# FFN gate and up of 18 of 22 tiles by seven products of quarters, with weight sums made by accumulating transfers

## The chip, the cores and the metric

The kernel runs on one core of a Trainium2 chip. The metric is the device time of one launch in microseconds; times are given as the median of several runs, and one further execution is recorded by the hardware profiler. Names used below: PE is TensorE (PEld its weight loads), DVE VectorE, ACT ScalarE, POOL GpSimd and SP SyncE, whose queue only starts transfers here.

## The reference

A decoder trunk of two layers on 512 tokens of 1024 channels: layer 0 mixes with a state-space model, layer 1 with stick-breaking attention; each is followed by the same kind of gated FFN, and a norm ends it. The change is in the FFN:

```
D_MODEL, SEQ, DEPTH, D_FF, CONV_W = 1024, 512, 2, 2816, 3

def conv_ffn(h, w_up, conv_w, conv_b, w_down):
    gu = h @ w_up
    g = gu[..., :D_FF]
    u = gu[..., D_FF:]
    g = conv_general_dilated(g, conv_w, padding=[(CONV_W - 1, 0)], feature_group_count=D_FF) + conv_b
    return (silu(g) * u) @ w_down

x = x + conv_ffn(rms_norm(x, norm_ffn[layer]), w_up[layer], conv_w[layer], conv_b[layer], w_down[layer])
```

## The kernel before

Everything is held channel by token: `x` is a tile of 128 partitions by 8 (the `k` of 1024 channels) by 512 tokens. A float32 product is made of three matmuls in fp32r: each operand is split into a high part (a cast by ACT, `split_hi`) and a low part (raw minus high, a DVE subtraction, `split_lo`), and `gemm` adds high x high, high x low and low x high in a bank of PSUM. Weights come from HBM into a `raw` tile (`load_raw`, by SP's queue), three of these in turn; their high and low parts have three buffers each (pool `wp`, tags `hi` and `lo`).

An FFN (`ffn`, `ffn_body`) has 22 tiles `f` of 128 hidden channels. For each, the gate's product `fg` and the up's `fu` run over 8 k with all 512 columns, 24 matmuls each. `rb` is the reciprocal root of the norm, one row per token; since the raw residual is what is multiplied (its high and low parts `xs`, made while the stage before ends), DVE multiplies `fg` and `fu` by `rb`. Then follow the causal convolution (`acc`: one ACT step, two DVE steps on 511 and 510 columns), silu on ACT (`s`), the product `u` and its split into `ah` and `al`, kept in `acts`. The 22 tiles go in three chunks of 8, 7 and 7 (`FF_CHUNKS`). After each chunk come eight downs `fd`, one per 128 output channels, each over the chunk's tiles, three matmuls a tile, and `x` gets `fd` added. After the last chunk of a layer each finished `x[:, n]` goes to the next stage (`st_next`); in layer 1 the last two downs are done by `Final.last` in halves of 256 tokens, in an order written by hand.

The order of the work on the engines is otherwise set by a scheduler, which puts an instruction ahead of others where it expects an operand sooner; each engine then runs its list strictly in order. Only in `Final.last`, and in the attention's loop, is the order that of the code. The seven banks of tag `b` are handed out in turn.

Of the kernel before, what the change touches and what calls it, by code (L numbers as in the profile page):

```python
# [47 lines left out]
def trunk(ctx: ExitStack, tc: tile.TileContext, A, out):  # L48
# [764 lines left out]


    def ffn(layer, prev, st_next):
        with Work(f"ff{layer}", {"g": "la", "s": "lb", "u": "lc"}, a=24, acc=2, y=1, half=6):
            banks_by_tag(b=7, st=1)
            rb, _ = prev.st.finish()
            ffn_body(layer, prev.xs, rb, st_next)

    def ffn_body(layer, xs, rb, st_next):
        cw = const.tile([P, FT, 4], F32, name="cw")
        nc.scalar.dma_start(out=cw, in_=A["conv"][layer])
        for ci, (f0, f1) in enumerate(FF_CHUNKS):
            acts = []
            for f in range(f0, f1):
                wg = load_split(A["w_up"][layer, f, 0], 8, name="wg")
                bg = B("fg")
                gemm(bg, wg, xs)
                wu = load_split(A["w_up"][layer, f, 1], 8, name="wu")  # L830
                bu = B("fu")
                gemm(bu, wu, xs)
                g = T("g", tag="g")
                tt(g, bg, rb, MUL)
                acc = T("acc", tag="acc")
                SC.activation(out=acc, in_=g, func=AF.Identity, scale=cw[:, f, 2:3], bias=cw[:, f, 3:4])  # L836
                stt(acc[:, 1:], g[:, :S - 1], cw[:, f, 1:2], acc[:, 1:], MUL, ADD)
                stt(acc[:, 2:], g[:, :S - 2], cw[:, f, 0:1], acc[:, 2:], MUL, ADD)
                s = T("s", tag="s")
                SC.activation(out=s, in_=acc, func=AF.Silu)  # L840
# [3 lines left out]
                ah, al = T("ah", F32R, "a"), T("al", F32R, "a")
                SC.copy(out=ah, in_=u)
                tt(al, u, ah, SUB)
                acts.append((ah, al))
            for n in range(KT):
                w = load_split(A["w_dn"][layer, n][:, f0 * P:f1 * P], f1 - f0, name="wd")
                if f1 == FT and n == KT - 2 and hasattr(st_next, "last"):  # L850
                    st_next.last((w, load_split(A["w_dn"][layer, KT - 1][:, f0 * P:f1 * P], f1 - f0, name="wd")), acts)
                    return
                bd = B("fd")
                gemm(bd, w, acts)
                tt(x[:, n], x[:, n], bd, ADD)
                if ci == len(FF_CHUNKS) - 1:
                    st_next(n)
# [498 lines left out]
    class Final:  # L1356
# [7 lines left out]
        def __call__(self, n):  # L1364
            self.st.add(n)
            if n == 0:
                tc.keep_in_program_order(SC.preload_act_table_set("abs_reciprocal_sqrt_and_small"))
                self.y = wide("yo", KT, "y").rearrange("p (k t) -> p k t", k=KT)
            SC.activation(out=self.y[:, n], in_=x[:, n], func=AF.Copy, scale=gcol(NFIN, n))

        def last(self, ws, acts):
            n0, H, K = KT - 2, S // 2, len(acts)
            halves = [slice(0, H), slice(H, S)]
            sq6, sq7, v, r, q, rr = (T(t, tag="half") for t in ("sq6", "sq7", "v7", "r7", "q7", "rr7"))
# [16 lines left out]

            def root(i):
                c = halves[i]
                SC.activation(out=r[:, c], in_=total[:, c], func=AF.Abs_reciprocal_sqrt, scale=1.0 / 1024.0, bias=self.eps)
# [134 lines left out]
```

## Time and profile before

| | |
|---|---|
| median of three runs | 1229.2 us (1228.55 to 1229.86) |
| the profiled execution: whole time | 1230.19 us |
| its span, first to last instruction | 1228.4 us |
| first FFN / second FFN in the chain of waits | 228.9 to 584.2 us / 866 to the end, about |
| TensorE clock granted, mean | 0.998 |
| transfers | 118.47 MB, 96 GB/s over the span |

The profile's views used below: the page (busy shares, the chain of waits by line, the costliest groups), the chain in order of time (start, length, engine, line and count), groups by shape (count, busy time, mean ns of one, idle time of the engine ahead of them and what ended it), windows (busy time of each engine in a stretch) and the timeline (start, length, instruction). A matmul's duration there is from its issue to its modelled end and overlaps the next; what a stream costs is read from start to start.

### The profile page before, as it was taken

The numbers are of one execution on the slowest core, as the hardware profiler recorded it, in microseconds if no ns is written. First come the engines' busy times: TensorE is split into PE (matmuls) and PEld (weight loads), VectorE is DVE, ScalarE is ACT, GpSimd is POOL, SyncE is SP. The second block draws the span as 40 slices with busy tenths as digits, with TensorE's granted clock in tenths as the row PEclk, the third lists the DMA queues.
The fourth block names the chain that finished last, engine by engine and source line by source line (L and its number), as shares of the span: only waits on it lengthen the run. The fifth ranks groups of instructions, "written<-read, shape, count | busy, mean of one in ns | idle before, by whom it ended". The sixth has DMA issues, their size and how long they took to land.

```text
span 1228.4 us, 16234 instructions
## 1 busy us (share of the span) xinstructions
PE 1204.6 (98%) x6434; PEld 984.1 (80%) x6434; DVE 804.0 (65%) x1254; ACT 546.0 (44%) x881; POOL 24.0 (2%) x65
## 2 busy tenths in 40 slices
PE   7999999999999999999999999999999999999996
PEld 3467788788888888888889898988888888888885
DVE  7999665655445635657878989878655346536554
ACT  5245453433223323334577878765433233313341
POOL 1011010000000000000000000000000000000000
PEclk9999999999999999999999999999999999999999
DMA  5565342223333233233211211123233332332322
GB/s 195 157 174 146 111 136 89 89 98 103 89 100 103 81 108 103 87 96 104 68 52 54 82 52 51 39 86 103 87 103 93 96 103 85 91 116 86 97 76 69
DMA packets 55037, 118.47 MB, mean 96 GB/s; under 512 B 12881, under 2 KB 28497, under 8 KB 54961
## 3 DMA queue, kind: packets, MB, share of 16 engines
q1 hardware_dynamic: 50304, 105.02, 28.2%
q0 software_dynamic: 3248, 11.54, 3.1%
q8 instruction: 50, 0.82, 0.3%
q10 hardware_dynamic: 1408, 0.88, 0.2%
q14 instruction: 27, 0.21, 0.1%
HBM read 109.03 MB, written 8.39 MB: 96 GB/s over the span
## 4 chain that ended last, share of the span: by engine, by line
PE 88%; DVE 8%; ACT 1%; issue 1%; DMA 1%; DVEq 0%; SPq 0%; ACTq 0%
PE fu L112 19%; PE fd L112 19%; PE fg L112 19%; PE gl L112 6%; PE kqb L112 6%; PE ob L112 5%; PE z L112 5%; PE v L112 4%; PE u L112 2%; DVE k L118 2%; DVE p L118 1%; PE y L112 1%; DMA x<-in_xT 1%; DVE cm L118 1%; ACT xg L282 1%
## 5 line engine op out<-in xcount | busy, mean ns | idle before, releaser
L112 PE MATMUL fd<-ah,wdh 128*128 128x512 f32 (+1 forms) x366 | 140.0, 382 | 0.0
L112 PE MATMUL fd<-al,wdh 128*128 128x512 f32 (+1 forms) x366 | 139.4, 381 | 0.0
L112 PE MATMUL fd<-ah,wdl 128*128 128x512 f32 (+1 forms) x366 | 139.4, 381 | 0.0
L118 DVE TENSOR_TENSOR x<-x,fd 128x512 f32<-128x512 f32 (+1 forms) x50 | 33.3, 665 | 116.6 <-PE fd L112 116.6
L163 ACT CAST wuh<-wur 128x1024 fp32r<-128x1024 f32 x44 | 46.3, 1053 | 134.0 <-PE fg L112 117.8
L163 ACT CAST wdh<-wdr 128x896 fp32r<-128x896 f32 (+1 forms) x48 | 47.2, 983 | 123.8 <-PE fd L112 91.5
L118 DVE TENSOR_TENSOR g<-fg,rb 128x512 f32<-128x512 f32 x44 | 30.4, 691 | 96.3 <-PE fg L112 93.6
L112 PE MATMUL fu<-xh,wuh 128*128 128x512 f32 x220 | 86.0, 391 | 0.0
L112 PE MATMUL fg<-xh,wgl 128*128 128x512 f32 x220 | 85.7, 389 | 0.0
L112 PE MATMUL fu<-xl,wuh 128*128 128x512 f32 x220 | 85.6, 389 | 0.0
L112 PE MATMUL fg<-xh,wgh 128*128 128x512 f32 x220 | 85.6, 389 | 0.0
L112 PE MATMUL fu<-xh,wul 128*128 128x512 f32 x220 | 85.6, 389 | 0.0
L112 PE MATMUL fg<-xl,wgh 128*128 128x512 f32 x220 | 85.6, 389 | 0.0
L118 DVE TENSOR_TENSOR u<-fu,rb 128x512 f32<-128x512 f32 x44 | 30.4, 691 | 80.5 <-PE fu L112 80.5
L112 PE MATMUL fu<-xhl,wuh 128*128 128x512 f32 x264 | 81.9, 391 | 0.0
L112 PE MATMUL fg<-xhl,wgh 128*128 128x512 f32 x264 | 81.6, 389 | 0.0
L112 PEld LDWEIGHTS fd<-ah,wdh 128*128 128x128 f32 x366 | 68.8, 188 | 13.3
L112 PEld LDWEIGHTS fd<-ah,wdl 128*128 128x128 f32 x366 | 68.8, 188 | 13.3
L112 PEld LDWEIGHTS fd<-al,wdh 128*128 128x128 f32 x366 | 68.8, 188 | 13.2
L163 ACT CAST wgh<-wgr 128x1024 fp32r<-128x1024 f32 x44 | 46.3, 1053 | 70.1 <-PE fd L112 32.6
L112 PE MATMUL u<-xg,wi 128*128 128x512 f32 x128 | 64.0, 635 | 7.3 <-ACT xg L282 7.3
L115 DVE SCALAR_TENSOR_TENSOR acc<-g,cw,acc 128x511 f32<-128x511 f32 x88 | 65.7, 747 | 2.5 <-ACT acc L836 0.9
(250 smaller groups left out, 2798.0 us busy)
## 6 DMA issues: line engine op xcount, KB each, us to landing
wgr<-in_w_up SPq DMA_DIRECT2D x44, 512.0 KB, 3.5
wur<-in_w_up SPq DMA_DIRECT2D x44, 512.0 KB, 3.5
wdr<-in_w_dn SPq DMA_DIRECT2D x32, 448.0 KB, 3.3
wdr<-in_w_dn SPq DMA_DIRECT2D x16, 512.0 KB, 3.5
wvr<-in_w_glu POOLq DMA_DIRECT2D x12, 512.0 KB, 3.8
ks<-kx SPq DMA_DIRECT2D x32, 128.0 KB, 2.5
m<-ks SPq DMA_DIRECT2D x8, 512.0 KB, 4.3
awr<-in_w_k SPq DMA_DIRECT2D x8, 512.0 KB, 3.4
```

The costliest lines, as they stand in the source:

```text
L112: PE.matmul(o, lhsT=lhsT, rhs=rhs, start=start, stop=stop, skip_group_check=True)
L115: (eng or V).scalar_tensor_tensor(out=o, in0=a, scalar=s, in1=b, op0=op0, op1=op1)
L118: (eng or V).tensor_tensor(out=o, in0=a, in1=b, op=op)
L163: SC.copy(out=hi, in_=raw)
L282: SC.activation(out=xg.rearrange("p (j c) -> p j c", j=8), in_=by_step(x[:, k]), func=AF.Copy, scale=gcol(NMIX0, k))
```

## The change

Four of the 22 tiles (the first chunk) are computed as before. The other 18 are computed by Strassen's scheme with seven products instead of eight. The 2x2 blocks are: rows gate and up, inner halves k 0 to 3 and k 4 to 7, columns tokens 0 to 255 and 256 to 511. Each of the seven products is 4 k x 3 matmuls of 256 columns (`prod`), two products a bank: `up1` and `gate2` in bank `f0`, `m17` and `n6` in `f1`.

- The seven sums of quarters of the activations, already normed (times gain and `rb`), are made once a layer by `make_forms(k)`, one call after each of the first chunk's four tiles, and split into `fh` and `fl` (DVE and ACT). They use the same three blocks (`block`, tag `sr`) that later hold the weight sums.
- The weight sums `wsa` and `wsb` are made by transfers (`summed`): SP's queue copies one quarter twice side by side into a block, and POOL's queue then adds the two diagonal quarters into it with an accumulating transfer, which waits for the copy. The diagonal quarters themselves (`wdg`) are a third transfer, and their difference `d` is a DVE subtraction. Each of `wsa`, `wdg`, `wsb` (1024 wide) and `d` (512 wide) is split into a high and a low part.
- The products are combined on DVE in halves of 256 (`t`, `wv`, `u`, `g`), with two copies from PSUM by ACT; no multiplication by `rb` is left in these tiles.
- The chunks are now 4, 5, 4, 5 and 4 tiles (`FF_ENDS`), so 40 downs a layer instead of 24 with the same number of matmuls. Three downs of the first chunk follow it at once (`LEAD`); the others stand between the products of the next chunk's tiles (`between`, twice a tile); the last chunk's eight come at the end.
- `acts` takes 8 buffers of its own and, in every other chunk, those of `xs` (tag `ta`). `Final` takes its tiles from the space of the forms, and `last` has its hand-written cuts moved, since the last chunk has 4 k instead of 7.

```
-FF_CHUNKS = ((0, 8), (8, 15), (15, 22))
+FF_ENDS = (4, 9, 13, 18, 22)
+LEAD = 3
...
+        def make_forms(k):
+            q, c = (block(n).rearrange("p (s c) -> p s c", s=4) for n in ("fq", "fc"))
+            for i, kk in ((1, k), (0, k + 4)):
+                stt(q[:, i::2], x[:, kk].rearrange("p (s c) -> p s c", s=2), gcol(NFFN0 if layer == 0 else NFFN1, kk),
+                    rb.rearrange("p (s c) -> p s c", s=2), MUL, MUL)
+            tt(c[:, 0:2], bc(q[:, 1], 1, [P, 2, H]), q[:, 2:4], ADD)
+            tt(c[:, 2], q[:, 3], q[:, 2], SUB)
+            tt(c[:, 3], q[:, 0], q[:, 2], ADD)
+            tt(q[:, 0], q[:, 0], q[:, 1], SUB)
+            for src, s in ((q[:, 0:3], slice(0, 3)), (c, slice(3, 7))):
+                SC.copy(out=fh[:, k, s], in_=src)
+                tt(fl[:, k, s], src, fh[:, k, s], SUB)
...
+            def summed(rows, half, name):
+                t = block(name)
+                t2 = t.rearrange("p (h c) -> p h c", h=2)
+                nc.sync.dma_start(out=t2, in_=quarters(rows, half, 0))
+                GP.dma_start(out=t2, in_=quarters(0, 0, diag), accum_op=ADD)
+                return t
...
+            def prod(o, wt, s, first=False, last=True):
+                gemm(o, wt, [(fh[:, k, s], fl[:, k, s]) for k in range(4)], k1=4, first=None if first else False, last=None if last else False)
+
+            s1 = split_w(summed(1, 0, "wsa"), 8, "wsa")
+            b0, b1 = B("f0"), B("f1")
+            up1, gate2, m17, n6 = b0[:, 0:H], b0[:, H:], b1[:, 0:H], b1[:, H:]
+            prod(up1, part(s1, 1), 1, True, False)
+            raw = wr.tile([P, 8 * P], F32, tag="raw", name="wdg", bufs=3)
+            nc.sync.dma_start(out=raw.rearrange("p (h c) -> p h c", h=2), in_=quarters(0, 0, diag))
+            r = split_w(raw, 8, "wdg")
+            prod(gate2, part(r, 0), 5, False, False)
+            d = fp.tile([P, S], F32, tag="d", name="d", bufs=1)
+            tt(d, raw[:, 0:4 * P], raw[:, 4 * P:], SUB)
...
+            prod(m17, (dh, dl), 3, True, False)
+            prod(n6, part(s1, 0), 4)
...
+            between(0)
+            prod(up1, part(r, 1), 0)
+            s2 = split_w(summed(0, 1, "wsb"), 8, "wsb")
+            prod(gate2, part(s2, 0), 2)
+            prod(m17, part(s2, 1), 6)
...
+            finish_act(f, g, mul, acts, tag)
+            between(1)
...
+            for f in range(f0, f1):
+                if ci == 0:
+                    up(f, acts, tag)
+                    make_forms(f)
+                else:
+                    up7(f, acts, tag, between)
+            todo = [(ci, n, acts) for n in range(KT)]
+            if ci == 0:
+                for _ in range(LEAD):
+                    down(*todo.pop(0))
```

How the instructions stand before and after is shown at three places. First, PE in an FFN, where a tile's gate ends and its up begins, before:

```order
L112 MATMUL fg<-xh,wgl 128x512
L112 MATMUL fg<-xhl,wgh 128x512 x2
L112 MATMUL fg<-xhl,wgl 128x512
L112 MATMUL fg<-xhl,wgh 128x512 x2
L112 MATMUL fg<-xhl,wgl 128x512
L112 MATMUL fg<-xhl,wgh 128x512 x2
L112 MATMUL fg<-xhl,wgl 128x512
L112 MATMUL fu<-xh,wuh 128x512
L112 MATMUL fu<-xl,wuh 128x512
L112 MATMUL fu<-xh,wul 128x512
```

And after, in the second tile of the second chunk, where the product `n6` (bank `f1`, here `f_2831`) ends and a down of the first chunk follows:

```order
L117 MATMUL f_2831<-fh,wsah 128x256
L117 MATMUL f_2831<-fl,wsah 128x256
L117 MATMUL f_2831<-fh,wsal 128x256
L117 MATMUL fd<-ah,wdh 128x512
L117 MATMUL fd<-al,wdh 128x512
L117 MATMUL fd<-ah,wdl 128x512
```

Matmuls of 512 columns have become matmuls of 256 with the same three parts, and a down now stands in the middle of a tile. Second, DVE in the first chunk, where no such work stood before; a tile there had, before, these rows (`wul` and `wgl` are low parts of weights, `al` of the activation):

```order
L118 TENSOR_TENSOR u<-u,s 128x512
L118 TENSOR_TENSOR wgl<-wgr,wgh 128x1024
L118 TENSOR_TENSOR al<-u,ah 128x512
L118 TENSOR_TENSOR g<-fg,rb 128x512
L118 TENSOR_TENSOR wul<-wur,wuh 128x1024
L115 SCALAR_TENSOR_TENSOR acc<-g,cw,acc 128x511
L115 SCALAR_TENSOR_TENSOR acc<-g,cw,acc 128x510
L118 TENSOR_TENSOR u<-fu,rb 128x512
```

and after, where the third tile's weights are split (`fq` and `fc` are the sums of quarters, `fl` their low parts):

```order
L123 TENSOR_TENSOR u_2410<-u_2410,s_2408 128x512
L123 TENSOR_TENSOR fc_2418<-fq_2417 128x256
L123 TENSOR_TENSOR wgl_2433<-wgr_2429,wgh_2431 128x1024
L123 TENSOR_TENSOR al_2414<-u_2410,ah_2413 128x512
L123 TENSOR_TENSOR fq_2417<-fq_2417 128x256
L123 TENSOR_TENSOR fl_2250<-fc_2418,fh_2249 128x1024
L123 TENSOR_TENSOR fl_2250<-fq_2417,fh_2249 128x768
L123 TENSOR_TENSOR wul_2464<-wur_2460,wuh_2462 128x1024
```

The steps of make_forms stand between those of the tile, the forms of the second call ahead of `wul`. Third, DVE in a seven-product tile of the second chunk:

```order
L123 TENSOR_TENSOR x<-x,fd 128x512
L123 TENSOR_TENSOR wsal<-wsa,wsah 128x1024
L123 TENSOR_TENSOR wdgl<-wdg,wdgh 128x1024
L123 TENSOR_TENSOR tw<-tw,f_2674 128x256 x2
L123 TENSOR_TENSOR g<-f_2675,tw 128x256
L123 TENSOR_TENSOR wdl<-wdr,wdh 128x512
L120 SCALAR_TENSOR_TENSOR acc<-g,cw,acc 128x511
L120 SCALAR_TENSOR_TENSOR acc<-g,cw,acc 128x510
L123 TENSOR_TENSOR tw<-f_2830,m_2892 128x256
L123 TENSOR_TENSOR u<-f_2674,s 128x256
L123 TENSOR_TENSOR u<-u,s 128x256
L123 TENSOR_TENSOR d<-wdg 128x512
```

The next tile's two low parts (`wsal`, `wdgl`) stand behind the addition to x and ahead of the steps that make this tile's gate (`tw`, `g`); `wsbl`, the last of the three, stands four rows further.

More of the change, by code (lines that the diff above doesn't have):

```diff
@@ L100, in wide, with forms_tile @@
         return pool.tile([P, n * S], F32, tag=tag, name=name, bufs=bufs[tag])
+    def forms_tile(name, dt=F32):
+        pool, bufs = cur["w"]
+        return pool.tile([P, 7 * 4 * (S // 2)], dt, tag="fo", name=name, bufs=bufs["fo"])
     def N(name, tag, bufs):
@@ L815, in ffn @@
     def ffn(layer, prev, st_next):
-        with Work(f"ff{layer}", {"g": "la", "s": "lb", "u": "lc"}, a=24, acc=2, y=1, half=6):
+        with tc.tile_pool(name=f"fd{layer}", bufs=1) as fp, \
+                Work(f"ff{layer}", {"g": "la", "s": "lb", "u": "lc"}, a=8, acc=2, fo=2):
             banks_by_tag(b=7, st=1)
             rb, _ = prev.st.finish()
-            ffn_body(layer, prev.xs, rb, st_next)
-    def ffn_body(layer, xs, rb, st_next):
+            ffn_body(layer, prev.xs, rb, st_next, fp)
@@ L822, in ffn_body, with block, finish_act, up @@
+    def ffn_body(layer, xs, rb, st_next, fp):
         cw = const.tile([P, FT, 4], F32, name="cw")
         nc.scalar.dma_start(out=cw, in_=A["conv"][layer])
[L824 to L840, printed above, removed]
+        H = S // 2
+        chunks = [(f, n) for f, n in zip((0,) + FF_ENDS, FF_ENDS)]
+        fh, fl = (forms_tile(n, F32R)[:, :7 * 4 * H].rearrange("p (k s c) -> p k s c", k=4, s=7) for n in ("fh", "fl"))
+        def block(name):
+            return fp.tile([P, 8 * P], F32, tag="sr", name=name, bufs=3)
+        def make_forms(k):
[10 more added lines that the diff above has]
+                tt(fl[:, k, s], src, fh[:, k, s], SUB)
+        def finish_act(f, g, mul, acts, tag):
+            acc = T("acc", tag="acc")
+            SC.activation(out=acc, in_=g, func=AF.Identity, scale=cw[:, f, 2:3], bias=cw[:, f, 3:4])
+            stt(acc[:, 1:], g[:, :S - 1], cw[:, f, 1:2], acc[:, 1:], MUL, ADD)
+            stt(acc[:, 2:], g[:, :S - 2], cw[:, f, 0:1], acc[:, 2:], MUL, ADD)
+            s = T("s", tag="s")
+            SC.activation(out=s, in_=acc, func=AF.Silu)
+            u = mul(s)
+            ah, al = T("ah", F32R, tag), T("al", F32R, tag)
+            SC.copy(out=ah, in_=u)
+            tt(al, u, ah, SUB)
+            acts.append((ah, al))
+        def up(f, acts, tag):
+            wg = load_split(A["w_up"][layer, f, 0], 8, name="wg")
+            bg = B("fg")
+            gemm(bg, wg, xs)
+            wu = load_split(A["w_up"][layer, f, 1], 8, name="wu")
+            bu = B("fu")
+            gemm(bu, wu, xs)
+            g = T("g", tag="g")
+            tt(g, bg, rb, MUL)
+            def mul(s):
@@ L843, in ffn_body @@
                 tt(u, u, s, MUL)
[L844 to L857, printed above, removed]
+                return u
@@ new lines, in up, with up7, quarters, part @@
+            finish_act(f, g, mul, acts, tag)
+        def up7(f, acts, tag, between):
+            w = A["w_up"][layer, f]
+            def quarters(rows, half, step):
+                o = w[rows, :, half * 4 * P:half * 4 * P + 4 * P]
+                return bass.AP(o.tensor, o.offset, [[KT * P, P], [step, 2], [1, 4 * P]])
+            diag = P * KT * P + 4 * P
+            def summed(rows, half, name):
[4 more added lines that the diff above has]
+                return t
+            def part(wt, h):
+                return [t[:, h * 4 * P:h * 4 * P + 4 * P] for t in wt]
+            def prod(o, wt, s, first=False, last=True):
[10 more added lines that the diff above has]
+            tt(d, raw[:, 0:4 * P], raw[:, 4 * P:], SUB)
+            dh, dl = (fp.tile([P, S], F32R, tag=n, name=n, bufs=2) for n in ("dh", "dl"))
+            SC.copy(out=dh, in_=d)
+            tt(dl, d, dh, SUB)
+            prod(m17, (dh, dl), 3, True, False)
+            prod(n6, part(s1, 0), 4)
+            m, tw, u = (T(n, tag="u") for n in ("m3", "tw", "u"))
+            t, wv = tw[:, 0:H], tw[:, H:]
+            SC.copy(out=m[:, 0:H], in_=gate2)
+            tt(t, up1, m[:, 0:H], ADD)
+            tt(wv, m17, t, ADD)
+            tt(u[:, H:], n6, wv, SUB)
+            between(0)
[3 more added lines that the diff above has]
+            prod(m17, part(s2, 1), 6)
+            g = T("g", tag="g")
+            tt(t, t, up1, SUB)
+            SC.copy(out=g[:, H:], in_=gate2)
+            tt(t, t, gate2, SUB)
+            tt(g[:, 0:H], m17, t, ADD)
+            def mul(s):
+                tt(u[:, 0:H], up1, s[:, 0:H], MUL)
+                tt(u[:, H:], u[:, H:], s[:, H:], MUL)
+                return u
+            finish_act(f, g, mul, acts, tag)
+            between(1)
@@ new lines, in down @@
+        def down(ci, n, acts):
+            f0, f1 = chunks[ci]
+            w = load_split(A["w_dn"][layer, n][:, f0 * P:f1 * P], f1 - f0, name="wd")
+            if f1 == FT and n == KT - 2 and hasattr(st_next, "last"):
+                st_next.last((w, load_split(A["w_dn"][layer, KT - 1][:, f0 * P:f1 * P], f1 - f0, name="wd")), acts)
+                return True
+            bd = B("fd")
+            gemm(bd, w, acts)
+            tt(x[:, n], x[:, n], bd, ADD)
+            if f1 == FT:
+                st_next(n)
@@ new lines, in ffn_body, with between @@
+        todo = []
+        for ci, (f0, f1) in enumerate(chunks):
+            acts, tag = [], ("a", "ta")[ci % 2]
+            slots = 2 * (f1 - f0)
+            n0, count = len(todo), [0]
+            def between(i):
+                count[0] += 1
+                while todo and (n0 - len(todo)) * slots < count[0] * n0:
+                    down(*todo.pop(0))
[8 more added lines that the diff above has]
+                for _ in range(LEAD):
+                    down(*todo.pop(0))
@@ L860, in attention @@
+        for job in todo:
+            if down(*job):
+                return
     def attention(prev, st_next):
@@ L1373, in last @@
             halves = [slice(0, H), slice(H, S)]
-            sq6, sq7, v, r, q, rr = (T(t, tag="half") for t in ("sq6", "sq7", "v7", "r7", "q7", "rr7"))
+            half = forms_tile("half")
+            sq6, sq7, v, r, q, rr = (half[:, i * S:i * S + S] for i in range(6))
             sq = {n0: sq6, n0 + 1: sq7}
@@ L1421, in last @@
                 mm(total[:, halves[0]], ones, acc[:, halves[0]], True, False)
-                product(n0, 1, 0, 5)
+                product(n0, 1, 0, 3)
                 mm(total[:, halves[0]], ones, sq[n0 + 1][:, halves[0]], False, True)
                 root(0)
-                product(n0, 1, 5, K)
+                product(n0, 1, 3, K)
                 newton(0)
@@ L1430, in last @@
                 send(0, 0, 4, nc.sync)
-                product(n0 + 1, 1, 0, 4)
+                product(n0 + 1, 1, 0, 2)
                 mm(total[:, halves[1]], ones, acc[:, halves[1]], False, False)
-                product(n0 + 1, 1, 4, K)
+                product(n0 + 1, 1, 2, K)
                 added(n0 + 1, 1)
```

2 lines of the change are left out of this document (1 added, 1 removed).

## The prediction

> **What bounds the kernel now.** I read the page's share table first, then the chain that ended last in order of time, then windows of the two kinds of FFN stretch, then groups by shape.
>
> ```profile
> span 1228.4 us, 16234 instructions
> PE 1204.6 (98%) x6434; PEld 984.1 (80%) x6434; DVE 804.0 (65%) x1254; ACT 546.0 (44%) x881; POOL 24.0 (2%) x65
> ...
> 312.24 43.52 PE fd L112 x192
> 355.76 5.44 PE fg L112 x24
> ...
> 708.04 5.76 PE v L112 x48
> ...
> 222.20:268.72 46.52, 46.03 (x204) 37.31 (x203) 29.76 (x48) 19.26 (x25) 0.00 (x0) 1.00 0.28 91
> ...
> 355.00:432.00 77.00, 77.00 (x342) 63.75 (x341) 43.80 (x55) 28.10 (x35) 0.00 (x0) 1.00 0.30 93
> ```
>
> In the FFN the chain never leaves TensorE: 24 products of 512 columns take 5.44 us and 192 take 43.52, so one costs **226.7 ns** start to start, at a granted clock of 1.00. (A matmul's duration in the groups is its whole life and overlaps the next.) In the window 355 to 432 (columns: length, PE, PEld, DVE, ACT, POOL, clock, DMA share, GB/s) PE is busy for all 77 us while DVE works 43.8, ACT 28.1 and the DMA engines are 0.30 busy. A saving on PE is therefore a saving of time until one of these reaches its own limit. The price of a 256-column product stands in the attention's v: 48 in 5.76 us, **120.0 ns**, so half the columns cost 53%, not 50%. These v matmuls also load a 128x128 weight each, so nothing is left of a doubt that the weight load would bound the narrower ones.
>
> **The change, part by part.**
>
> *PE.* Before, a tile's gate and up take 48 x 226.7 ns = 10.88 us. After, seven products of 4 k x 3 = 12 matmuls of 256 columns: 84 x 120.0 ns = 10.08 us. That is 0.80 us a tile, and 36 tiles (18 in each of two layers) give **-28.8 us**. The count of down matmuls is the same; they only move.
>
> The Trainium skill, "TensorE: Matmul & The Clock Gate", section "Back-to-back issue gap", gives 262 cycles for 256 columns and 518 for 512 at 2.4 GHz. By it a tile would save 48 x 518 - 84 x 262 = 2856 cycles, 1.19 us, and the 36 tiles 42.8 us. The trace has 120.0 ns where that table has 109, and 226.7 where it has 216, so the trace disagrees by 11 ns on each; the fixed part weighs more on 84 short matmuls, and the sum goes by the trace.
>
> *DVE, first chunk of each layer: make_forms.* It must fit beside four unchanged tiles.
>
> ```profile
> 263.28 5.44 PE fu L112 x24
> ...
> 235.55 0.69 DVE L118 TENSOR_TENSOR g<-fg,rb 128x512 f32<-128x512 f32 x1 [1.90 <-ACT rb L228]
> ...
> 238.14 1.53 DVE L115 SCALAR_TENSOR_TENSOR acc<-g,cw,acc 128x511 f32<-128x511 f32 x2
> ...
> 378.35 0.69 DVE L118 TENSOR_TENSOR u<-u,s 128x512 f32<-128x512 f32 x1
> 378.96 1.22 DVE L118 TENSOR_TENSOR wgl<-wgr,wgh 128x1024 fp32r<-128x1024 f32 x1
> 380.10 0.68 DVE L118 TENSOR_TENSOR al<-u,ah 128x512 fp32r<-128x512 f32 x1
> ...
> 1213.13 0.42 DVE L124 TENSOR_SCALAR v<-sum 128x256 f32<-128x256 f32 x1 [2.74 <-ACT r L1394]
> 1213.47 0.41 DVE L115 SCALAR_TENSOR_TENSOR q<-r 128x256 f32<-128x256 f32 x1
> ```
>
> Start to start DVE needs 0.61 us for 512 elements, 1.14 for 1024, 0.34 for 256 (0.42 where the next waits on it), 0.76 for a conv step. One call of make_forms is two steps of 2x256 with a scalar (0.68 each, estimated between 0.61 and 0.76), one of 512, three of 256, a low part of 768 (0.88, between) and one of 1024: 5.0 us, four calls 20. Nothing of it can start before rb, in this trace at 235.5. The first seven-product tile could start when four tiles (the fourth's fu ends at 268.7) and three downs of K = 4 are through: 268.7 + 36 x 0.2267 = 276.9. So DVE has 41.4 us for: forms 20.0; g, u, u*s, al of four tiles 16 x 0.61 = 9.8; four conv pairs 6.1; four low weight parts 4.6; three low parts of downs and two additions to x 3.1; d and the first wsa 1.8. Sum 45.3. It is **3.9 us late**, and the DVE order after shows where: the low part of the third gate weight stands behind the forms, and PE's rows there break into pieces of two matmuls. Twice: **+8 us** (from 0, if the early low parts and the last additions fit outside this stretch, to 12, if the late ones queue again behind the other layer's start).
>
> *DVE and ACT, a seven-product tile.* The tightest is the second chunk: five tiles with one down of K = 4 each, period 10.08 + 12 x 0.2267 = 12.80 us.
>
> ```profile
> L118 DVE TENSOR_TENSOR wgl<-wgr,wgh 128x1024 fp32r<-128x1024 f32 x44 | 53.7, 1220 | 10.3 <-ACT wgh L163 10.1
> L118 DVE TENSOR_TENSOR u<-u,s 128x512 f32<-128x512 f32 x44 | 30.4, 690 | 4.6 <-ACT s L840 1.0
> L115 DVE SCALAR_TENSOR_TENSOR acc<-g,cw,acc 128x511 f32<-128x511 f32 x44 | 32.8, 744 | 0.9 <-ACT acc L836 0.9
> L118 DVE TENSOR_TENSOR x<-x,fd 128x256 f32<-128x256 f32 x4 | 1.7, 419 | 2.3 <-PE fd L112 2.3
> L163 ACT CAST wgh<-wgr 128x1024 fp32r<-128x1024 f32 x44 | 46.3, 1053 | 70.1 <-PE fd L112 32.6 <-PE fu L112 28.1 <-PE gl L112 8.9
> L836 ACT ACTIVATE acc<-g,cw 128x512 f32<-128x512 f32 x44 | 35.7, 811 | 0.8 <-DVE g L118 0.8
> L845 ACT CAST ah<-u 128x512 fp32r<-128x512 f32 x44 | 27.4, 623 | 37.7 <-DVE u L118 37.7
> L840 ACT ACTIVATE s<-acc 128x512 f32<-128x512 f32 x44 | 27.8, 632 | 86.7 <-DVE acc L115 86.7
> ```
>
> DVE has three low parts of 1024 (3.66), eight halves of 256 (3.35), two conv steps (1.49) and five of 512 (d, dl, al, x, wdl; 3.45): 11.95 us by whole durations, 10.7 start to start, of 12.80. ACT: three casts of 1024 (3.16), acc (0.81), s, ah, dh and the down's cast (0.63 each) and two copies of 256 (under 0.63 each): below 7.8. Both fit. What is short is one loop: there are three hi and three lo buffers, and the next tile's wsa takes the pair of wdg, whose last matmul starts at 5.76 + 2.72 + 1.44 = 9.92 us of the period. Cast 1.05 and low part 1.22, with 0.16 for the matmul to end and some 0.1 of handing over, end at 12.4; PE wants the low part at 12.80 + 0.24. Slack 0.6 us. Behind a late low part on DVE stand wdgl and g's own steps, so one delay would pass on. I take **0**: every part has a measured duration and the order stands as needed; the far end is 1 us for each of the ten tiles of these chunks. The other chunks have 14.4 to 16.9 us a period.
>
> *Chunk ends and x.* Sixteen more additions to x a layer are in the DVE sum. Where a chunk ends, the last gate's g (0.42), acc (0.81), conv steps (1.49), s (0.63), u (0.42), ah (0.62) and al (0.69) make 5.1 us, with an addition to x and the hand-overs some 6.3; a down and nine matmuls (5.4) or four products and nine (7.8) cover it. Only the layer's end is short: **+1 us** for both.
>
> *The tail.*
>
> ```profile
> 1209.93 0.43 PE sum L112 x2
> 1210.36 1.79 PE fd L112 x15
> ...
> 1216.79 1.08 PE fd L112 x9
> ```
>
> The last chunk has 4 instead of 7 k. 18 matmuls of 512 (4.1 us) go ahead of the tail; 18 of 256 leave its first half (2.2) and 18 its second, where 15 and 9 in these rows become 9 and 6 but the DVE chain behind the sums stays: about 1.1 of 2.2. **+1 us** (0 to 2).
>
> *Transfers.* A tile now loads 2.6 MB instead of 1.05, and two of its five 512 KB transfers accumulate, issued by POOL once the first copy has landed.
>
> ```profile
> wgr<-in_w_up SPq DMA_DIRECT2D x44, 512.0 KB, 3.5
> ...
> wvr<-in_w_glu POOLq DMA_DIRECT2D x12, 512.0 KB, 3.8
> ...
> L143 POOL DMA_DIRECT2D wvr<-in_w_glu x16 | 8.5, 533 | 77.9 <-DVE wvl L118 50.0 <-ACT mt L655 19.6 <-DVE kx L115 5.2
> ...
> 7.00:17.00 10.00, 8.62 (x11) 2.37 (x10) 8.94 (x74) 8.81 (x10) 0.00 (x0) 1.00 1.00 391
> ```
>
> Plain, a sum lands 3.5 + 0.5 + 3.8 = 7.8 us after its buffer is free; the three blocks give it 13.6 us in the second chunk (from wsb's low part at 9.5 to two periods less 2.5). The window at the start shows 391 GB/s with every engine busy. A tile of the second chunk moves 1.84 MB plain and 1.05 accumulated: if an accumulated byte costs m plain ones, (1.84 + 1.05 m) / 0.391 = 4.7 + 2.7 m us of 12.8. No row shows m. From below it is 1 (7.4 us, hidden), nothing makes it less; hidden until 3.0. I take the nearest row, the plain POOL transfer, and **0**.
>
> By the Trainium skill, "Collectives: The Full Stack", section "The bandwidth ceiling: the fold count and why AG ≠ RS ≠ AR", an add in the DMA engine reads two sources and runs at half a copy's rate; m = 2 would be 10.1 us of 12.8 and the sum would stay. No run here shows it yet.
>
> **Sum.** -28.8 + 8 + 1 + 1 = -18.8. The profiled execution took 1230.2 (span 1228.4 and 1.8 around it), 1.0 above the median shown; from the median, 1229.2 - 18.8 = **1210 us**.
>
> **Rivals.**
> 1. *The forms hide after all* (DVE catches up, PE finds other matmuls): 1229.2 - 28.8 + 2 = 1202. For it: the scheduler already put other matmuls into the gap. Against: 45.3 in 41.4.
> 2. *The seven-product tiles wait for their low parts.* The loop with 0.6 us of slack slips, by 1 us in each of ten tiles: 1220; up to 1227 if the other 26 slip by 0.25 us. For: DVE at 84 to 93% there. Against: DVE is no slower beside POOL's transfers in the stage before (wvl, in the rows below, against wgl's 1220).
> 3. *Slower: the accumulating transfers bound the tile.* From m = 3 the second chunk is bound by its transfers; at 4 its tiles take 15.4 instead of 12.8 and those of the fourth 15.8 instead of 14.4, (5 x 2.6 + 5 x 1.4) x 2 = 40: 1250. It cancels the gain at about 3.6. For: no accumulating transfer is in the trace. Against: a factor near 4 is needed.
> 4. *The saving isn't there* (256 columns dearer than 120 ns with other operands): at 129.5 ns it is nil, 1239. Against: fd's own matmuls of 256 columns, with the operands of the FFN, have v's 283 ns.
>
> ```profile
> L112 PE MATMUL v<-awh,xl 128*128 128x256 f32 x80 | 22.7, 283 | 0.0
> ...
> L112 PE MATMUL fd<-al,wdh 128*128 128x256 f32 x28 | 7.9, 283 | 0.0
> ...
> L118 DVE TENSOR_TENSOR wvl<-wvr,wvh 128x1024 fp32r<-128x1024 f32 x15 | 18.2, 1220 | 16.7 <-ACT wvh L163 16.7
> ```
>
>
> **How the numbers follow.** Forecast (1205 to 1216) 0.54, rival 1 0.12, rival 2 0.14, rival 3 0.17, rival 4 0.03. The measurement tells 0.2% (2.5 us) from no change; I count 0.03 within it, out of rivals 2 to 4. Faster 0.79, same 0.03, slower 0.18. The range leaves out the far part of rival 3 and what lies under the forms hidden whole: 1200 to 1236.
>
> **What would show it.** Right: f0 and f1 at 120 ns start to start; PE full in the seven-product tiles; some 4 us of PE waiting for DVE between the third gate and the first wsa of each layer; DVE near 90% in the second chunk; a sum landing in 8 to 11 us. Wrong: PE idle before wsah or wsbh with the accumulating transfer as releaser (rival 3), or before wsal with DVE or ACT (rival 2).

## The result, and the profile after

| | before | after |
|---|---|---|
| median | 1229.13 us (1228.55 to 1229.86, 4 runs) | 1266.59 us (1262.46 to 1270.37, 4 runs) |
| ratio after to before | | 1.0304, 95% interval 1.0261 to 1.0346 |
| profiled execution, whole time | 1230.19 us | 1269.93 us |
| its span | 1228.4 us | 1268.2 us |

The changed kernel is slower by 37 us; 1210 was forecast, and the range (1200 to 1236) did not hold the time. The page of after, first: span, TensorE's share, the chain that ended last, the costliest rows of PE's and DVE's waiting, POOL's queue (packets, MB, share of the 16 engines' span) and the issues (count, size, median us from issue to landing).

```profile
span 1268.2 us, 19862 instructions
PE 1203.6 (95%) x7712; PEld 1037.4 (82%) x7712; DVE 978.4 (77%) x1670; ACT 641.5 (51%) x1073; POOL 109.1 (9%) x137
...
q0 software_dynamic: 22832, 49.29, 20.4%
...
PE 71%; DVE 15%; DMA 9%; ACT 3%; issue 2%; DVEq 0%; SPq 0%; ACTq 0%
...
L117 PE MATMUL f<-fh,wsbl 128*128 128x256 f32 x288 | 85.8, 298 | 19.3 <-DVE wsbl L123 19.3
L123 DVE TENSOR_TENSOR d<-wdg 128x512 f32<-128x512 f32 x36 | 24.9, 692 | 102.0 <-DMA wdg<-in_w_up 102.0
L117 PE MATMUL f<-fh,wdgl 128*128 128x256 f32 x288 | 83.8, 291 | 6.8 <-DVE wdgl L123 6.8
L117 PE MATMUL f<-fh,wsah 128*128 128x256 f32 x288 | 82.6, 287 | 4.8 <-ACT wsah L168 4.8
...
wdg<-in_w_up SPq DMA_DIRECT2D x36, 512.0 KB, 6.6
wsa<-in_w_up SPq DMA_DIRECT2D x36, 512.0 KB, 3.5
wsa<-in_w_up POOLq DMA_DIRECT2D x36, 512.0 KB, 8.1
wsb<-in_w_up SPq DMA_DIRECT2D x36, 512.0 KB, 5.1
wsb<-in_w_up POOLq DMA_DIRECT2D x36, 512.0 KB, 8.0
```

PE's busy time fell by 1 us where 28.8 were to be saved (part of it ran at a lower clock: the mean granted clock is 0.980, where it was 0.998), and it is idle for 41 us more. PE itself waits most for low parts that DVE makes, 19.3 us for `wsbl` and 6.8 for `wdgl`; what DVE waits for is the question. The largest of DVE's waits is a small one repeated: `d`, the difference of the diagonal quarters, a DVE step of 0.69 us, stood 102 us in all for the plain transfer `wdg`, which lands in 6.6 us where the two plain copies of the same size on SP's queue land in 3.5 (`wsa`) and 5.1 (`wsb`). An accumulating transfer lands in 8.

The chain in order of time (start, length, engine, line) shows where, in the first FFN:

```profile
252.30 8.04 PE fg L117 x22
...
281.49 9.60 DMA wdg<-in_w_up
...
293.05 6.51 DMA wdg<-in_w_up
307.23 6.84 DMA wdg<-in_w_up
323.12 8.11 DMA wdg<-in_w_up
334.53 4.86 PE f L117 x21
340.83 7.14 DMA wdg<-in_w_up
...
362.68 10.07 PE f L117 x84
```

The price on which the gain rested is right: 84 products of 256 columns in 10.07 us, 119.9 ns each. What is new is transfers of `wdg` that each end a wait: one at the start of the second chunk (281.49, 9.60 us long), then four, 14 to 18 us apart, in that chunk, whose tiles PE needs only 12.8 us for. (Two more, at 461.00 and 491.17, stand in the fourth chunk.) Two timelines, DVE's and SP's, show how one leads to the next (start, length, instruction, and in brackets the idle time ahead and its releaser):

```profile
306.52 0.68 DVE L123 TENSOR_TENSOR wdl<-wdr,wdh 128x512 fp32r<-128x512 f32 x1
314.09 0.69 DVE L123 TENSOR_TENSOR d<-wdg 128x512 f32<-128x512 f32 x1 [3.49 <-DMA wdg<-in_w_up]
...
322.42 0.68 DVE L123 TENSOR_TENSOR wdl<-wdr,wdh 128x512 fp32r<-128x512 f32 x1
331.25 0.69 DVE L123 TENSOR_TENSOR d<-wdg 128x512 f32<-128x512 f32 x1 [4.76 <-DMA wdg<-in_w_up]
```

```profile
307.23 0.37 SPq L912 DMA_DIRECT2D wdg<-in_w_up  x1
...
323.12 0.37 SPq L912 DMA_DIRECT2D wdg<-in_w_up  x1
```

`wdl`, the low part of a down's weight, frees a `raw` buffer at 307.2 (306.52 + 0.68); SP, which has waited for it, issues `wdg` at 307.23; it lands some 7 us later; `d`, next on DVE's list, starts at 314.09; the steps behind it lead to the next `wdl` at 322.42, and that to the next `wdg` at 323.12. The loop takes 16 to 18 us, 7 to 8 of them the transfer. The low part `wsbl`, for which PE waits, comes behind `d` on DVE's list (at 316.09 and 333.26 in the chain).

The windows (length, PE, PEld, DVE, ACT and POOL busy, granted clock, DMA share, GB/s) show a second part of the price:

```profile
250.00:260.00 10.00, 7.70 (x22) 6.11 (x23) 7.65 (x11) 2.40 (x3) 0.00 (x0) 0.66 0.25 79
290.00:300.00 10.00, 9.87 (x54) 9.57 (x55) 6.00 (x11) 2.75 (x5) 1.28 (x2) 0.71 0.76 197
330.00:340.00 10.00, 5.90 (x29) 5.70 (x28) 7.78 (x12) 3.42 (x5) 1.18 (x1) 0.66 0.51 137
...
355.00:430.00 75.00, 74.99 (x520) 69.88 (x519) 56.94 (x94) 36.06 (x52) 11.81 (x10) 1.00 0.84 204
```

Around and after these gaps of PE the mean granted clock of a 10 us window is 0.66 to 0.71, so up to 3.4 us of full clock (10 x 0.34) were lost beside the gap itself; the last section shows that not every gap had this effect. From 355 to 430, in the third chunk's longer tiles, PE is full, as forecast, with the DMA engines 0.84 busy.

### The profile page after: what moved, and what is told of

Its sections match the earlier page's. It is cut to its first block, busy times and chain, and to the rows that moved or that the text cites. A ratio compares the mean times of both kernels' runs of the same rounds, so it can differ in the third digit from the quotient of the medians.

```text
span 1268.2 us, 19862 instructions
## 1 busy us (share of the span) xinstructions
PE 1203.6 (95%) x7712; PEld 1037.4 (82%) x7712; DVE 978.4 (77%) x1670; ACT 641.5 (51%) x1073; POOL 109.1 (9%) x137
## 4 chain that ended last, share of the span: by engine, by line
PE 71%; DVE 15%; DMA 9%; ACT 3%; issue 2%; DVEq 0%; SPq 0%; ACTq 0%
PE f L117 22%; PE fd L117 15%; DMA wdg<-in_w_up 7%; PE gl L117 6%; PE kqb L117 5%; PE ob L117 5%; PE z L117 4%; PE fg L117 3%; PE v L117 3%; PE fu L117 2%; PE u L117 2%; DVE k L123 2%; DVE p L123 1%; DVE wsbl L123 1%; DVE wdgl L123 1%
## 5 line engine op out<-in xcount | busy, mean ns | idle before, releaser
L117 PE MATMUL f<-fh,wsbl 128*128 128x256 f32 x288 | 85.8, 298 | 19.3 <-DVE wsbl L123 19.3
L123 DVE TENSOR_TENSOR d<-wdg 128x512 f32<-128x512 f32 x36 | 24.9, 692 | 102.0 <-DMA wdg<-in_w_up 102.0
L117 PE MATMUL f<-fh,wdgl 128*128 128x256 f32 x288 | 83.8, 291 | 6.8 <-DVE wdgl L123 6.8
L117 PE MATMUL f<-fh,wsah 128*128 128x256 f32 x288 | 82.6, 287 | 4.8 <-ACT wsah L168 4.8
L117 PE MATMUL f<-fh,wsbh 128*128 128x256 f32 x288 | 84.1, 292 | 0.0
L117 PE MATMUL f<-fl,wsbh 128*128 128x256 f32 x288 | 84.1, 292 | 0.0
L117 PE MATMUL f<-fh,wdgh 128*128 128x256 f32 x288 | 82.9, 288 | 0.3 <-DVE tw L123 0.3
L117 PE MATMUL f<-fl,wdgh 128*128 128x256 f32 x288 | 83.0, 288 | 0.0
L117 PE MATMUL f<-fh,wsal 128*128 128x256 f32 x288 | 82.5, 286 | 0.5 <-DVE wsal L123 0.5
L117 PE MATMUL f<-fl,wsah 128*128 128x256 f32 x288 | 82.4, 286 | 0.0
L117 PEld LDWEIGHTS fd<-al,wdh 128*128 128x128 f32 x360 | 67.9, 188 | 13.6 <-DVE al L123 2.4
L117 PEld LDWEIGHTS f<-fh,wsbl 128*128 128x128 f32 x288 | 58.2, 202 | 21.7 <-DVE wsbl L123 21.7
L918 ACT CAST dh<-d 128x512 fp32r<-128x512 f32 x36 | 22.3, 621 | 97.6 <-DVE d L123 97.6
```

The source lines that it names most:

```text
L117: PE.matmul(o, lhsT=lhsT, rhs=rhs, start=start, stop=stop, skip_group_check=True)
L123: (eng or V).tensor_tensor(out=o, in0=a, in1=b, op=op)
L918: SC.copy(out=dh, in_=d)
```

## The experiments

Theory: the time is lost in that loop (a shared raw buffer, then `wdg`'s transfer, then `d` at the head of DVE's list), which closes because the accumulating transfers load the DMA engines and stretch `wdg`'s landing; and, apart from it, in the first seven-product tile of each layer, whose sum is made too late. Rivals: the accumulating transfers are themselves too slow; there are too few buffers whatever the load; the chunking; the forms.

**e1, buffers of its own for wdg.**

```
-            raw = wr.tile([P, 8 * P], F32, tag="raw", name="wdg", bufs=3)
+            raw = TB("wdg")
```

> The changed kernel with wdg in three buffers of its own (tag tb, free once the first chunk's xs are used), so that the raw buffers serve the downs' weights alone and wdg's transfer no longer waits for the low part of a down's weight. Loop theory (the low part wdl frees a raw buffer, then wdg's transfer of 6.6 us, then d at the head of DVE's list, then the next wdl): the waits of d for wdg, 102 us in 32 pieces, fall below 30, the second chunk's tiles go from 17 us back towards 12.8, and the time falls from 1266.6 to 1215-1235. Rival, rate (the accumulating transfers and their sums are late themselves): the waits move from wdg to wsa and wsb and the time stays at 1255-1270. Rival, chunking or forms: no change beyond 5 us.

1235.3 us (one execution) beside 1230.5 of before: 31 us gone, a hair over the upper end of the expected 1215 to 1235. The group of `d` in this run:

```profile
L123 DVE TENSOR_TENSOR d<-wdg 128x512 f32<-128x512 f32 x36 | 24.8, 689 | 22.2 <-DMA wdg<-in_w_up 22.0
```

The wait fell from 102 to 22 us with all transfers as before, still landing in 6.3 and 8.5 us. That speaks for the loop and against the bare rate of the transfers.

**e2 and e3, plain transfers, and none.**

```
-                GP.dma_start(out=t2, in_=quarters(0, 0, diag), accum_op=ADD)
+                GP.dma_start(out=t2, in_=quarters(0, 0, diag))
```

That is e2's edit; in e3 the line is left out. Both kernels thus leave the weight sums out.

> The changed kernel with POOL's 72 transfers as plain copies into the same blocks (the second copy overwrites the first, so the weight sums are left out). Same bytes, same order, same buffers. Loop theory with accumulating as its cause: POOL's 49.3 MB cost about 27 instead of 49 us of engine time a transfer, wdg lands in 4-5 us instead of 6.6, the waits of d fall below 40 us and the time is 1215-1240. Rival, bytes (what loads the engines is 2.6 MB a tile, however written): wdg still lands in over 6 us and the time stays over 1250. Rival, too few raw buffers whatever the load: the same, over 1250.

> The changed kernel without POOL's 72 transfers (the weight sums are left out, the first copy stands for them). Loop theory closed by transfer load: wdg lands in 3.5-4 us, the loop takes some 12.5 us, under the 12.8 of a tile of the second chunk, d hardly waits, the first tile starts at about 281; what is left of the cost is the stall behind the forms (8 for both layers) and chunk ends, so 1208-1220. Rival, too few raw buffers whatever the load: over 1240. Rival, chunking, DVE or forms bound it: over 1240.

1234.5 and 1215.5 us. `d` waited 47.5 and 23.5 us, `wdg` landed in 5.0 and 4.0. With the shared buffers left as they were, taking away the load opens the loop too, so "too few buffers whatever the load" falls: both are needed. And e2 prices accumulating, from POOL's queue in e2 and in before:

```profile
q0 software_dynamic: 13616, 49.29, 12.2%
```

```profile
q0 software_dynamic: 3248, 11.54, 3.1%
```

Shares of 16 engines' spans: e2 0.122 x 16 x 1232.7 = 2406 us of engine time, before 609, so 1797 / 72 = **25.0 us** for a plain transfer of 512 KB; after 0.204 x 16 x 1268.2 = 4139, so 3530 / 72 = **49.0 us** for an accumulating one. The factor that I called m is **1.96**. The Trainium skill, "Collectives: The Full Stack", section "The bandwidth ceiling: the fold count and why AG ≠ RS ≠ AR", says of the add in a collective (ReduceScatter) that it needs two source reads and so runs at half a copy's rate; for these accumulating transfers the trace agrees.

**e4, e14 and e15, the chunking alone** (all tiles by the eight products of before).

```
-                if ci == 0:
-                    up(f, acts, tag)
-                    make_forms(f)
-                else:
-                    up7(f, acts, tag, between)
+                up(f, acts, "a")
+                if ci:
+                    between(0)
+                    between(1)
...
-FF_ENDS = (4, 9, 13, 18, 22)
+FF_ENDS = (8, 15, 22)
```

The last two lines are e14's alone, which also has the cuts in `last` as before the change; in e4 and e15 the acts have 18 buffers, in e14 30.

> All 22 tiles by the eight products of before (no forms, no sums), but in chunks of 4, 5, 4, 5 and 4 with the downs between the tiles, as in the changed kernel; the acts have 18 buffers. Loop theory: chunking and interleaving cost next to nothing by themselves, 1229-1234 (sixteen more additions to x and downs a layer, beside PE). Rival, chunking or interleaving is the cost: over 1245, with PE waiting at chunk ends.

> All 22 tiles by the eight products of before, in chunks of 8, 7 and 7 as before, but with the downs between the next chunk's tiles (three at once after the first chunk). If e4's 6.6 us come from the short last chunk (less matmul time behind which the attention's start and the tail are prepared): 1228-1231. If they come from the interleaving: 1234-1238.

> The kernel of e4 again, with an interval: 1234-1238 if its one look was right.

e4 1237.1, e15 1237.4 (ratio to before 1.0053, interval 1.0037 to 1.0068), e14 1230.5 (0.9998, 0.9982 to 1.0014). So interleaving costs nothing that these runs resolve, and the short chunks 6.5 us, where I had 2 and had expected 1229 to 1234 of e4. The FFN itself is not longer for it; windows of the attention's start, e4 and then before:

```profile
600.00:640.00 40.00, 37.62 (x209) 32.71 (x209) 30.42 (x52) 28.03 (x55) 0.00 (x0) 0.96 0.16 51
```

```profile
600.00:640.00 40.00, 40.00 (x240) 35.86 (x239) 31.19 (x53) 29.67 (x59) 0.00 (x0) 1.00 0.18 54
```

PE is full there before, and idle for 2.4 us in e4. In e4 and in e15 2.2 us of it is one wait of the attention's `z` for a step of ACT (`w`, line 1228); before has no such wait there.

**e5 to e7, the sums on POOL's adder.** A tile then loads 1.05 MB, as before the change.

```
+                tt(t2, r2, bc(off[:, half * 4 * P:half * 4 * P + 4 * P], 1, [P, 2, 4 * P]), ADD, GP)
-                nc.sync.dma_start(out=t2, in_=quarters(rows, half, 0))
-                GP.dma_start(out=t2, in_=quarters(0, 0, diag), accum_op=ADD)
...
-            tt(d, raw[:, 0:4 * P], raw[:, 4 * P:], SUB)
+            tt(d, raw[:, 0:4 * P], raw[:, 4 * P:], SUB, GP)
...
-            tt(c[:, 2], q[:, 3], q[:, 2], SUB)
+            tt(c[:, 2], q[:, 3], q[:, 2], SUB, GP)
```

The step `d` moves in e6 and e7, the forms' sums (this line and three like it) in e7 alone. `r2` is `wdg` in buffers of its own, `off` a raw tile with the two other quarters.

> The weight sums made by GpSimd's adder instead of accumulating transfers: a tile loads its two diagonal quarters (wdg, in buffers of its own) and its two other quarters (one raw tile) once, 1.05 MB as before the change, and POOL adds a quarter to both diagonal ones, 1024 elements, twice a tile. Loop theory: with 118 MB in all, no accumulating and no shared buffer, wdg lands in about 3.5 us, d waits under 25 us in all and the time is 1208-1222, if a POOL sum takes under 5 us (two of them under 10 of the 12.8 us of a tile). Rival, POOL: a sum takes over 6 us, then POOL bounds the second and fourth chunks and the time is over 1240. Rival, DVE slows beside POOL: the low parts' mean rises from 1.22 us by over 15%, DVE fills the 12.8 us, and the time is 1230-1250.

> As e5, and d (the difference of the diagonal quarters) also on POOL, so that DVE no longer stands behind wdg's transfer for it. Loop theory: 0 to -5 us against e5, since with e5's transfers d hardly waits. Rival, d at the head of DVE's list is the cost whatever the transfers do: -10 us or more against e5. If POOL bounds: +5 us or more.

> As e6, and four of the eleven DVE steps of make_forms (the sums and differences, about 1.6 us a call by DVE's prices) also on POOL. My step on the forms (DVE 3.9 us late in the first chunk of each layer, PE idle and then at a lower clock): DVE has 6.4 us less there, the stall before the third gate goes, and the time falls by 5-8 us against e6, to 1203-1215. Rival: the stall is set by the latency of the chain through the forms, longer on POOL: no gain or a loss.

1270.7, 1265.8 and 1274.8 us. Of e5 and e7 my expectation failed; e6 against e5, -4.8 us, is what I had expected of it. (A call of make_forms has eight DVE steps; I wrote eleven.) The rival that DVE slows beside POOL held, at a higher price than it had (1230 to 1250). A POOL sum takes 2.6 (`wsa`) to 2.9 us (`wsb`) in the mean, well under 5. But the low part `wsal`, in e1 and then in e5, rose by half:

```profile
L123 DVE TENSOR_TENSOR wsal<-wsa,wsah 128x1024 fp32r<-128x1024 f32 x36 | 44.1, 1224 | 32.4 <-ACT wsah L168 32.1
```

```profile
L123 DVE TENSOR_TENSOR wsal<-wsa,wsah 128x1024 fp32r<-128x1024 f32 x36 | 65.5, 1820 | 5.5 <-ACT wsah L168 5.5
```

And two timelines of e5, POOL's and DVE's, lie like this:

```profile
378.90 2.86 POOL L123 TENSOR_TENSOR wsb<-wdg,wod 128x1024 f32<-128x1024 f32 x1
...
397.57 2.85 POOL L123 TENSOR_TENSOR wsb<-wdg,wod 128x1024 f32<-128x1024 f32 x1
```

```profile
379.54 2.77 DVE L120 SCALAR_TENSOR_TENSOR acc<-g,cw,acc 128x510 f32<-128x510 f32 x1
...
398.08 0.67 DVE L123 TENSOR_TENSOR x<-x,fd 128x512 f32<-128x512 f32 x1
398.68 2.43 DVE L123 TENSOR_TENSOR wdl<-wdr,wdh 128x640 fp32r<-128x640 f32 x1
```

The conv step (0.74 us elsewhere) ends at 382.31, 0.55 after POOL's sum at 381.76; `wdl` (0.8) ends at 401.11, 0.69 after POOL's at 400.42: each waited for POOL's whole instruction. `x<-x,fd`, which reads one operand from PSUM, ran beside it in its usual 0.67. In all, POOL's sums take 198 us in e5, and DVE's busy time is 1084.5 us where it is 982.6 in e1: DVE's steps grew by about half of the adder's time, and DVE was 80% busy already. The Trainium skill, "SBUF — State Buffer", section "SBUF: two separate sides", tells of such an exclusive lock, against a DVE step with two SBUF inputs; the trace agrees.

The lock need not be the whole price. `off` sits in the shared `raw` buffers, so a loop is closed here too: SP issues the next `wod` when POOL's second sum ends (at 303.61, 319.05 and 334.79), and `wdg` behind it at 304.09, 319.50 and 335.28, 15 to 16 us apart. What the slower DVE costs and what this loop costs was not separated.

**e8, e1 once more.**

> The kernel of e1 again (wdg in buffers of its own, accumulating transfers): how far one look repeats. Expected 1235 within 4 us.

1236.2 us, beside e1's 1235.3.

**e9 and e12, the first sums early.** e1's first tile still waited, by PE's timeline:

```profile
286.67 0.58 PE L117 MATMUL f<-fh,wsah 128*128 128x256 f32 x1 [5.72 <-ACT wsah L168]
```

In after the same place shows SP's issue of the copy, POOL's of the addition, and ACT's first cast of the sum:

```profile
273.14 0.46 SPq L897 DMA_DIRECT2D wsa<-in_w_up  x1
```

```profile
278.52 1.22 POOL L898 DMA_DIRECT2D wsa<-in_w_up  x1 [84.72 <-DMA wsa<-in_w_up]
```

```profile
287.78 1.04 ACT L168 CAST wsah<-wsa 128x1024 fp32r<-128x1024 f32 x1 [9.49 <-DMA wsa<-in_w_up]
```

The three blocks for the sums serve the forms' temporaries first, so the copy comes late, behind the downs' weights and the first `wdg` in SP's list; the sum lands 9.3 us after POOL's issue, and the cast starts at 287.78 where I had the first tile's products at 276.9. The edit gives the temporaries the place that `dh` and `dl` use later (e9 has it and e1's edit, e12 it alone):

```
-            q, c = (block(n).rearrange("p (s c) -> p s c", s=4) for n in ("fq", "fc"))
+            q, c = (pair(n).rearrange("p (s c) -> p s c", s=4) for n in ("fq", "fc"))
...
-            dh, dl = (fp.tile([P, S], F32R, tag=n, name=n, bufs=2) for n in ("dh", "dl"))
+            dd = pair("dd", F32R)
+            dh, dl = dd[:, 0:S], dd[:, S:]
...
+        def pair(name, dt=F32):
+            return fp.tile([P, 2 * S], dt, tag="dd", name=name, bufs=2)
```

> e1 with the temporaries of make_forms moved out of the three blocks of the weight sums into two tiles that dh and dl use later, so that the first sums can be loaded and accumulated while the first chunk still runs. Theory: in e1 the first seven-product tile of each layer waits for its sum (PE idle 5.7 us in layer 0, the accumulating transfer lands 10.3 us after its issue, the clock falls after it); that goes, twice, 16-20 us with the clock: 1235 becomes 1214-1221. Rival, rate: the transfers are late in every tile, the start only shifts them, and the time stays at 1228-1236.

> The changed kernel with only the forms' temporaries moved (as in e9), wdg still in the shared raw buffers. If the loop over the raw buffers and the late first sum are separate costs, this takes 10-20 off 1266.6, to 1247-1257, and the loop's waits of d for wdg stay over 80 us. Rival, the late first tile starts the whole pile-up: under 1235, with d's waits under 40 us.

e9 1215.5 us (1215.16 to 1221.76), ratio 0.9879, interval 0.9852 to 0.9906: 1.2% shorter than before, and 51 us shorter than after. e12 1251.8, with `d` waiting 97.6 us. So the two costs are separate and nearly add: 15 us for the first tile, 31 for the loop, 51 for both together. With its sums, e9 takes no longer than e3 without them.

**e10, more downs ahead of the first tile** (`LEAD = 5` in e9).

> e9 with five instead of three downs of the first chunk before its first seven-product tile (three left for the next five tiles), so that DVE gets 5.4 us more for the forms and the second chunk's tiles have fewer downs to prepare. Theory: e9's remaining stall is the forms, in the middle of the first chunk, which later downs do not move, so -3 to +1 against e9. Rival, the lateness of 3.9 us is what is lost, wherever it stands: -4 us or more.

1231.9 us, ratio 1.0017 (1.0001 to 1.0033): 16 slower than e9, against both expectations. A window that lies mostly in the second chunk, e9 and then e10:

```profile
290.00:360.00 70.00, 69.73 (x517) 66.64 (x516) 58.88 (x98) 36.84 (x54) 12.96 (x11) 1.00 0.89 217
```

```profile
290.00:360.00 70.00, 64.95 (x488) 62.57 (x487) 54.16 (x88) 35.57 (x51) 12.69 (x11) 0.98 0.89 214
```

The transfers run at the same share, 0.89, and nearly the same rate. By the sum, the rate could be what binds here: a tile of the second chunk takes three plain transfers, two accumulating ones and a down's weight, 3 x 25.0 + 2 x 49.0 + 12.5 = 185 us of engine time (if SP's plain transfers cost what POOL's do), 11.6 us of 16 engines, and 13.0 at the share of 0.89. With one down a tile PE needs 12.8 us, as much; with three downs for five tiles it needs 10.08 + 0.6 x 2.72 = 11.7, and the transfers, (185 - 0.4 x 12.5) / 16 / 0.89 = 12.6, can't follow. That is 0.9 us for each of ten tiles, and e10 lost 16. A rival is the latency, as in the loop; e10's chain in this window has

```profile
299.86 7.78 DMA wdg<-in_w_up
314.40 7.57 DMA wdg<-in_w_up
...
340.31 8.16 DMA wsa<-in_w_up
```

Which of the two it is was not tried.

**e11, e1 and e2 together.**

> e1 and e2 together: wdg in buffers of its own and POOL's transfers plain (the weight sums are left out). Loop theory: either edit alone opens the loop (each took 31-32 us), and what both leave, the late first tile, is shortened by the plain transfer only: 1222-1230. Rival, the two are separate costs that add: 1203-1212.

1221.8 us, a hair under the lower end, with `d` waiting 3.5. The two edits took 31 and 32 us alone and 45 together, not 63: for the most part they take away the same thing, as the loop theory has it.

**e13, one form of four** (in e9).

```
-                    make_forms(f)
+                    if f == 0:
+                        make_forms(f)
...
-                gemm(o, wt, [(fh[:, k, s], fl[:, k, s]) for k in range(4)], k1=4, first=None if first else False, last=None if last else False)
+                gemm(o, wt, [(fh[:, 0, s], fl[:, 0, s]) for k in range(4)], k1=4, first=None if first else False, last=None if last else False)
```

> e9 with the forms of k = 0 alone, used for every k (three of four calls of make_forms are left out, some 15 us of DVE time in each first chunk). My term for the forms was +8 for both layers: 1215.5 becomes 1206-1210. Rival, the forms cost little once the sums are early: 1213-1216.

1214.2 us, ratio 0.9855 (0.9831 to 0.9878), beside 0.9879 of e9; the intervals overlap. The expected 1206 to 1210 was missed and the rival held: the forms cost little.

One table puts the profiles side by side. A stage is taken from the start of its first `stat` or `kqb` matmul to that of the next (us); `d` is the time that it waited for `wdg`. The time is the median; of e1, e2, e3 and e12 there is one execution. The stretch ahead of the first FFN, which no edit touches, takes 226.8 to 232.3 us in these profiles (232.3 in e9's, 229.3 in e13's), so the stages are the surer measure of a few microseconds.

| | first FFN | attention | second FFN | d waits | time |
|---|---|---|---|---|---|
| before | 356.2 | 272.4 | 372.0 | | 1229.1 |
| after | 372.9 | 275.3 | 391.1 | 102.0 | 1266.6 |
| e12 early sums | 364.9 | 275.2 | 379.5 | 97.6 | 1251.8 |
| e1 own buffers | 358.0 | 275.5 | 371.5 | 22.0 | 1235.3 |
| e2 plain | 357.8 | 275.5 | 369.2 | 47.5 | 1234.5 |
| e3 no sums | 348.2 | 274.8 | 362.3 | 23.5 | 1215.5 |
| e9 both | 349.1 | 275.0 | 363.6 | 8.1 | 1215.5 |
| e13 one form | 344.8 | 275.4 | 362.8 | 16.4 | 1214.2 |
| e15 chunks | 356.5 | 275.1 | 374.6 | | 1237.4 |
| e14 three chunks | 356.2 | 272.5 | 372.0 | | 1230.5 |

## Why the prediction was wrong, step by step

**PE, -28.8: right.** The price is 119.9 ns, and long stretches run at it without a gap.

**Transfers, 0: the step that failed.** e3 leaves the sums' transfers out and takes 1215.5; after takes 1266.6: 51 us that I had at nothing. The step compared two rates and one lead: what a tile's transfers take (7.4 us at m = 1) against its period, and the sum's landing against its 13.6 us. Two sizes in it were wrong: m is 1.96, not 1, and plain transfers on POOL's queue ran at 336 GB/s (512 KB in 25.0 / 16 us), not at 391, so that a tile takes 11.6 of 12.8 us. But even that is under the period, so rival 3, the bare rate, is not what e1 to e3 show for this kernel. At such a load a transfer lands later (`wdg` in 6.6 us instead of 3.5), and one of them had no lead: `wdg` can be issued only when the low part of a down's weight gives back a raw buffer, and DVE waits for it at the head of its list before it can make the next such low part. I worked out the lead for the sums, and never for the third transfer, nor for the first tile's sum, which stands behind the forms' temporaries in the same blocks. e1 (the loop), e2 (the load that closes it) and e12 (the first tile) show each part.

**Forms, +8: right in its place, too large.** The third gate's `wgl` did stop PE, at 252.30 with 2.6 us idle, where I put it. But with the first sums early (e9 against e13), three forms of four are worth 4.2 us in the first FFN, 0.8 in the second, and 1.4 by the medians. The 4.2 is about what the gap (2.6) and the lower clock after it (1.7, at 0.83 over 10 us) make in e9. The second FFN has no such stall (the windows from 880 to 920 of after have PE busy for all 40 us), so "twice" was wrong.

**Steady tiles, 0: right.** In e3 PE is busy 39.7 to 40 of every 40 us from 260 to 580, with DVE at 31 to 36. The sign of rival 2, PE waiting for low parts, is on the page of after, but not its cause: in e9, with the same low parts to make, PE waits 0.6 us in all for `wsbl`, where it waited 19.3.

**Chunk and layer ends +1, tail +1: too small.** e15 gives 6.5 us: 2.7 in the attention and 2.6 in the second FFN. I looked for the layer's end in the FFN and not in the stage behind it. What makes ACT's `w` late there was not tried.

**Rivals 1 and 4.** Rival 4 (dear products) is excluded by the rows. Rival 1 (1202) was not reached even by e13.

**What is left.** e9 gains 15.6 us on before, near the 18.8 of the forecast, and part of that is luck: forms priced too high and chunks too low cancel. With -28.8 for PE, 6.5 for the chunks and 1.4 to 5.0 for the forms, e9 should have gained 17 to 21; the 2 to 5 us between stay open.

## What to carry to other kernels

A transfer that fits by its rate can still set the pace: follow each one from what frees its buffer to who stands at the head of an in-order list for it, and ask whether that list also frees the buffer, with the landing time under the new load rather than the old. A temporary that borrows the buffers of a prefetch takes the prefetch away just where the stage begins.

## What the runs showed of the hardware

- An accumulating transfer took 1.96 times the engine time of a plain one of the same bytes (49.0 against 25.0 us for 512 KB, from the queue's shares in after and e2), and landed in 8.0 to 8.1 us beside 5.3 to 5.7 for the plain one at the same place (e2).
- A plain transfer of 512 KB landed later where the DMA engines were busier: `wdg` in 4.0 us in e3, where their share from 290 to 430 us is 0.45, in 5.0 in e2 (0.64), and in 6.0 in e9 (0.86); before, a weight landed in 3.5 at 0.31.
- In e5, a DVE step with both operands in SBUF ended only after POOL's whole addition (2.77 us instead of 0.74), while a DVE step with one operand in PSUM did not wait: `x<-x,fd` took 0.680 us in the mean, 0.684 in e1.
- The same gap of PE did not always lower its clock. In nine profiles PE waited 2.60 or 2.61 us for one low part in the first chunk of the first FFN. Over the 10 us from the start of that gap the granted clock was 0.66 in after and e8, 0.83 in e3, e9 and e12, and 1.00 in e1, e2, e10 and e11; e1 and e8 are the same kernel. So this gap cost between nothing and 3.4 us (10 x 0.34) beside its own length, and the kernel alone did not decide which. The window of e1 around its gap at 249.31:

```profile
220.00:260.00 40.00, 36.87 (x162) 29.10 (x161) 32.26 (x59) 17.90 (x23) 0.00 (x0) 1.00 0.20 60
```
